# A first stage ordered by a list scheduler, with five more chunks of q in it, and an output projection by input quarters

## The chip, the cores and the metric

The kernel runs on one core of a Trainium2 chip. A core has TensorE (PE, matmuls; its weight loads are listed as PEld), VectorE (DVE), ScalarE (ACT), GpSimd (POOL) and SyncE (SP), each with an instruction stream of its own that it works off strictly in order, and 16 DMA engines fed from queues; here SP's queue carries the weights, POOL's some small transfers. The metric is the device time of one execution in microseconds, the median of several runs. Matmuls accumulate into PSUM, of which the kernel uses eight banks of 128 partitions x 512 float32.

## The reference

One encoder layer over 256 tokens of width 2048, all in float32. Only the attention mixer is used (the depth is 1).

```python
mod = silu(c) @ mod_w + mod_b                          # 2048 x 12288, one row c
sh_m, sc_m, g_m, sh_f, sc_f, g_f = split(mod, 6)
h = x * (1 + sc_m) + sh_m
q, k, v = split(h @ w_qkv + b_qkv)                      # 2048 x 3072: 32 q heads, 8 k and 8 v heads of 64
q, k = rope(q), rope(k)
s = where(|qpos - kpos| <= 128, q @ k.T / 8, -inf)      # four q heads share one k and v head
m = max(s.max(), sink); p = exp(s - m)
o = (p / (p.sum() + exp(sink - m))) @ v
x = layer_norm(alpha * x + (1 + g_m) * (o @ w_o + b_o)) # w_o: 2048 x 2048
h = x * (1 + sc_f) + sh_f
y = square(relu(h @ w1 + b1)) @ w2 + b2                 # 2048 -> 8192 -> 2048
out = layer_norm(alpha * x + (1 + g_f) * y)
```

## The kernel before

**Numbers and chunks.** Every large product is made of three matmuls in a reduced float32 format (`mm3`, L556): the high half of the activation by the high half of the weight (L557), high by low (L558), low by high (L559). Weights come in chunks of 128 x 2048 float32 (1 MB). A chunk of weights is split in two pieces of 1024 columns: ScalarE rounds a piece to the tile `wh` (L291), VectorE takes the difference to the raw chunk, `wl` (L262). The activations hold their halves in `g` tiles (`held`, pairs `hh, hl`).

**Stream.** `Stream` (L218) holds one list of chunks in the order in which they are loaded, all from SP's queue. There are eight raw buffers (`raws`, five, and three early ones, `raws2`, given up later), five `wh` and five `wl` tiles. `loads` asks for the next chunks while buffers are free; `pump` rounds and subtracts ahead as far as the tiles allow; `main` gives the next chunk's halves; `done` marks a half as used. A raw buffer comes free when its second low half is made or, for a chunk of modulation weights, when its product is.

**Modulation.** The 2048 x 12288 product with one row has 96 chunks. A row product puts the chunk through PE (`quad`, L346, PSUM tile `pm`), after which ScalarE copies the row out (`mrow`, L375) and PE turns it (`pt`, L426; for the gate L460 and L462). A column product is one VectorE instruction over the whole chunk (L386; `cb` holds the spread c). `MIXP` says which of the 16 groups of 128 inputs have their scale and shift by rows (ten groups, two chunks each), the rest by columns; `FFP` says it for the feed-forward's four groups. `columns` adds the bias, and `modulated` (L578) makes h of 128 inputs: one ScalarE instruction and two of VectorE.

**First stage.** q, k and v are six columns of 512 outputs (`CORD`): k, q0, v, q1, q2, q3. The first three, `p` = 0 to 2, are 12 chunks, each of four units (`UNITS`: 128 inputs of one column), accumulated in six PSUM banks (`sums`, two token tiles of three columns). Between them stand the 32 chunks of modulation for x. The order is written out by hand as letters: u a unit, g a modulation product, m a `modulated`, p a pump. With `S.pin` set the instructions keep this order on their engines. Each column gets its bias through a matmul (`bq`, L207) and is copied out (`evict`). PE has some instructions without use at the start (`idle`).

**Slots.** The other 12 q chunks (`LATE`, columns q1, q2, q3, four input groups each) run over two banks for a column. Three (`PRE`) come before the first scores, between them the rotation and the transposes of k and q0. Then come 25 slots: 0 to 8 have a q chunk each, 9 to 24 a chunk of the output projection. Slots 0 to 15 also hold one step of attention each, with four heads and one token tile: `scores` (L744), which VectorE masks and reduces (L751) and ScalarE puts through the exponential (L761); `normalise` (L776); `probs_T`, the transposes of the probabilities (L786); and in each second slot `values` (L802, with L806 for the low half). `SLOT_FILL` says how many chunks of modulation (gate rows, then the feed-forward's groups) are placed at each slot.

**Output projection.** `project(js, c)` (L844) makes 512 outputs from two input quarters (`oT[j]`: eight heads), so from two chunks in two slots. The eviction adds the bias (L888) for the first half of the inputs, and for the second adds to the first (L890), multiplies with the gate and adds x (L892 to L895). The last, `c` = 3, runs token tile by token tile, with the statistics and the normalisation behind each (`add_gated` L811, `norm_scalars`, `normed` L837, L842). The gate gets to the rows' form by `m_gm.spread` at slot 13: a row (`grow`, L475) goes out to DRAM (L476) and comes back on all partitions (L478), both by POOL's queue. `project_0(3)` at slot 20 applies it to a part that is done by then. After this comes the feed-forward, with W1 and W2 in four blocks.

## Time and profile before

| | us |
|---|---|
| median of 3 runs | 1116.48 (1114.97 to 1117.6) |
| profiled execution | 1114.57 |
| its span | 1112.8 |
| PE busy in the span | 1071.0 (96%) |
| VectorE busy | 761.2 (68%) |
| ScalarE busy | 522.9 (47%) |
| mean granted clock of PE | 0.986 of full |

The trace is of one execution, and its times count from the span's start. The stages in it: the first ends at 134.9, the first scores start at 156.7, the feed-forward begins at about 373. A row such as "L262 DVE wl<-raw,wh" tells line, engine, output tile and input tiles; "pa" are PSUM banks for products, "pt" for transposes, "pm" for modulation rows, "g" the general tiles of 128 x 1024. In a table of stretches, each engine's busy time stands with the number of its instructions, "PEclk" is the granted clock, "DMA share" how busy the 16 DMA engines were. In a list of waits the numbers are total us, count, and the longest one. Where an instruction's row ends in brackets, they hold the idle time ahead of it and what ended it.

### The profile page before, as it was taken

To read this page: it belongs to the slowest core of one execution; us is meant where nothing else is said; L and a number is where in the kernel's file an instruction comes from. 1 tells how busy PE (TensorE), PEld (TensorE's weight loads), DVE (VectorE), ACT (ScalarE), POOL (GpSimd) and SP (SyncE) were. 2 spreads that over 40 slices of the span, in tenths; PEclk is the share of its full clock that TensorE was granted. 3 is DMA by queue.
4 is the path that set the end of the run, shared out by engine and by line. 5 is a ranking of instruction groups with operands and counts; after the bars stand their busy time and mean duration, and the time that the engine had idled before them with its cause. 6 is when DMAs were issued, how large, how long until landed. Compare 5 with 4: busy or idle time off the path is not lost.

```text
span 1112.8 us, 15919 instructions
## 1 busy us (share of the span) xinstructions
PE 1071.0 (96%) x6377; PEld 880.0 (79%) x6377; DVE 761.2 (68%) x1098; ACT 522.9 (47%) x811; POOL 21.4 (2%) x42
## 2 busy tenths in 40 slices
PE   8887999899999998999999999999999999999995
PEld 5655677677678798988888888888888888888884
DVE  2576688888548687765578878766666556665576
ACT  2333447888743446553444443334444344444340
POOL 2000000000000000000000000000000000000001
PEclk9998999999999999999999999999999999999998
DMA  9999989878697698555677777876555555557522
GB/s 377 419 420 420 419 299 343 305 293 302 227 386 258 272 361 312 189 190 189 229 282 284 294 287 246 304 269 224 190 189 189 189 191 189 188 189 265 189 76 76
DMA packets 43835, 292.74 MB, mean 263 GB/s; under 512 B 5060, under 2 KB 5220, under 8 KB 9968
## 3 DMA queue, kind: packets, MB, share of 16 engines
q1 hardware_dynamic: 40400, 281.83, 68.1%
q0 software_dynamic: 2496, 8.43, 2.4%
q10 hardware_dynamic: 864, 1.45, 0.4%
q8 instruction: 50, 0.82, 0.3%
q14 instruction: 25, 0.20, 0.0%
HBM read 289.58 MB, written 2.11 MB: 262 GB/s over the span
## 4 chain that ended last, share of the span: by engine, by line
PE 83%; DVE 8%; ACT 3%; DMA 3%; issue 2%; POOL 0%; SPq 0%; DVEq 0%; ACTq 0%; POOLq 0%
PE pa L1077 16%; PE pa L558 15%; PE pa L559 14%; PE pa L557 14%; PE pa L1078 8%; PE pm L346 3%; PE pa L1053 3%; DVE wl L262 3%; PE pa L1054 3%; PE pa L1055 3%; DVE raw L386 2%; DMA raw<-in_wqkv 1%; ACT wh L291 1%; PE pa L744 1%; PE pa L802 1%
## 5 line engine op out<-in xcount | busy, mean ns | idle before, releaser
L262 DVE TENSOR_TENSOR wl<-raw,wh 128x1024 fp32r<-128x1024 f32 x332 | 402.6, 1222 | 240.1 <-ACT wh L291 239.0
L291 ACT CAST wh<-raw 128x1024 fp32r<-128x1024 f32 x332 | 346.0, 1051 | 390.0 <-PE pa L559 220.1
L558 PE MATMUL pa<-wl,g 128*128 128x512 f32 x816 | 321.9, 395 | 8.8 <-DVE wl L262 8.5
L557 PE MATMUL pa<-wh,g 128*128 128x512 f32 x816 | 319.6, 397 | 7.6 <-ACT wh L291 5.8
L559 PE MATMUL pa<-wh,g 128*128 128x512 f32 x816 | 319.2, 393 | 0.0
L1077 PE MATMUL pa<-g,wh 128*128 128x512 f32 x768 | 271.6, 399 | 0.0
L1078 PE MATMUL pa<-g,wl 128*128 128x256 f32 x768 | 215.7, 281 | 0.0
L557 PEld LDWEIGHTS pa<-wh,g 128*128 128x128 f32 x816 | 152.5, 188 | 47.9 <-ACT wh L291 8.0
L558 PEld LDWEIGHTS pa<-wl,g 128*128 128x128 f32 x816 | 154.7, 190 | 43.9 <-DVE wl L262 12.5
L559 PEld LDWEIGHTS pa<-wh,g 128*128 128x128 f32 x816 | 154.5, 190 | 33.3 <-issue 0.8
L1077 PEld LDWEIGHTS pa<-g,wh 128*128 128x128 f32 x768 | 144.3, 188 | 36.2 <-issue 0.2
L1078 PEld LDWEIGHTS pa<-g,wl 128*128 128x128 f32 x768 | 145.1, 189 | 0.1
L386 DVE CUSTOM_DVE_ANT_0 raw<-raw,cb 128x2048 f32<-128x2048 f32 x52 | 118.2, 2283 | 10.1 <-DMA raw<-in_mod 10.1
L1053 PE MATMUL pa<-g,wh 128*128 128x256 f32 x256 | 73.0, 288 | 4.5 <-ACT wh L291 4.5
L1055 PE MATMUL pa<-g,wl 128*128 128x256 f32 x256 | 72.8, 287 | 0.1
L1054 PE MATMUL pa<-g,wh 128*128 128x256 f32 x256 | 72.3, 285 | 0.0
L1053 PEld LDWEIGHTS pa<-g,wh 128*128 128x128 f32 x256 | 49.4, 194 | 5.4 <-ACT wh L291 5.4
L1054 PEld LDWEIGHTS pa<-g,wh 128*128 128x128 f32 x256 | 49.2, 193 | 0.9 <-DVE b L914 0.7
L1055 PEld LDWEIGHTS pa<-g,wl 128*128 128x128 f32 x256 | 49.4, 193 | 0.4 <-DVE wl L262 0.3
L346 PE MATMUL pm<-raw,cact 128*32 128x128 f32 (+1 forms) x1024 | 47.0, 324 | 0.9 <-DMA raw<-in_mod 0.8
L346 PEld LDWEIGHTS pm<-raw,cact 128*32 128x32 f32 x1024 | 28.0, 112 | 19.4 <-issue 11.7
L761 ACT ACTIVATE g<-g,nm 128x256 f32<-128x256 f32 x64 | 31.8, 499 | 16.8 <-DVE nm L751 16.7
(180 smaller groups left out, 659.5 us busy)
## 6 DMA issues: line engine op xcount, KB each, us to landing
raw<-in_mod SPq DMA_DIRECT2D x96, 1024.0 KB, 7.9
raw<-in_w SPq DMA_DIRECT2D x64, 1024.0 KB, 4.9
raw<-in_w1b SPq DMA_DIRECT2D x48, 1024.0 KB, 4.9
raw<-in_wqkv SPq DMA_DIRECT2D x24, 1024.0 KB, 12.7
raw<-in_wo SPq DMA_DIRECT2D x16, 1024.0 KB, 7.5
raw<-in_w1a SPq DMA_DIRECT2D x16, 1024.0 KB, 7.2
g<-in_x SPq DMA_DIRECT2D x4, 512.0 KB, 8.5
gb<-in_lnrow POOLq DMA_DIRECT2D x8, 256.0 KB, 5.7
```

What stands on the lines that cost most here:

```text
L262: self.pinned(nc.vector.tensor_sub(l, r, f32(self.hs[n])))
L291: self.pinned(nc.scalar.copy(h, s))
L346: i = nc.tensor.matmul(self.ps[32 * j:32 * j + 32, :w], lhsT[j] if type(lhsT) is list else lhsT, rhs[j], start=self.first, stop=stop)
L386: S.pinned(nc.vector.tensor_tensor_reduce(out=raw, in0=raw, in1=cb, scale=1.0, scalar=0.0, op0=OP.mult, op1=OP.add, accum_out=self.dst))
L557: nc.tensor.matmul(ps, xh, wh, start=start, stop=False)
L558: nc.tensor.matmul(ps, xh, wl, start=False, stop=False)
L559: S.prev = nc.tensor.matmul(ps, xl, wh, start=False, stop=stop).ins
L1053: nc.tensor.matmul(o, wh(w, 128), hh, start=new, stop=False)
L1054: nc.tensor.matmul(o, wh(w, 128), hl, start=False, stop=False)
L1055: nc.tensor.matmul(o, wl(w, 128), hh, start=False, stop=end)
L1077: nc.tensor.matmul(ps, wh(k, 128), hb, start=k == 0, stop=False)
L1078: nc.tensor.matmul(ps[:, :256], wl(k, 128), hb[:, :256], start=False, stop=k == NK - 1)
```

## The change

1. *The first stage's order comes from a list scheduler.* `first_order` has a cost in us for each kind of operation, what each must wait for, and the times at which the loads would land by its own model (2.47 us a chunk, eight buffers). It takes again and again the operation that could start first, and by rank among equals. The kernel then emits the operations in that order, all pinned: g a modulation product, r, c and a the row's copy, transpose and bias, H, T and S the three instructions of `modulated` (T now writes a tile of its own, `xm`), h and l a high and a low half, u a unit, e an eviction, sp and cp the spread of c.
2. *Five more chunks run in it.* `SEQ` has the 12 chunks and, as pairs (input group, column), (0,3), (0,4), (1,3), (1,4), (2,3): three quarters of q1 and two of q2. The modulation rows share one bank (`gv`), which frees the eighth bank for these: a quarter and token tile is accumulated, then evicted, by ScalarE as a copy for group 0 and by VectorE as an addition after it (`add_part`). `spread` uses this bank too.
3. *Seven chunks are left behind it* (`LATE`), two of them ahead of the slots, and there are 21 slots instead of 25: q chunks in slots 0 to 4, the projection in 5 to 20. The later parts of q1 and q2 are added to `acc` on VectorE.
4. *The output projection goes by input quarters,* `project(c, j)`, one chunk and one slot each, j outermost. Each is evicted: j = 0 with the bias (L1058), 1 and 2 by addition, 2 with the gate and x behind it (`project_0`, L1069 and L1070), 3 by `add_gated`, which is now the end of all four columns. The last one has 12 matmuls for each token tile, where 24 stood.
5. *What hangs on slot numbers moves.* The gate's spread goes to slot 11 (was 13), the rows of x to 11 (was 15), the first feed-forward columns to 17 (was 19); `SLOT_FILL` is new. `FFP` becomes (2, 2, 4, 0). The rotary tables are made ahead of the stage.

```diff
-PRE = 3
-OUT_AT = 9
-X_AT = 15
+PRE = 2
+OUT_AT = 5
+X_AT = 11
+SLOT_FILL = (1, 1, 1, 1, 1, 1, 1, 2, 2, 2, 2, 2, 2, 2, 2, 2, 2, 2, 2, 2, 1, 0, 0)
...
-FFP = (0, 4, 4, 0)
+FFP = (2, 2, 4, 0)
...
+SEQ = [(0, [1, 2]), (1, [3]), (2, []), ((0, 3), [4]), ((0, 4), [5]), (3, [6]), (4, [7]), (5, []),
+       ((1, 3), [8]), ((1, 4), [9]), (6, [10]), (7, [11]), (8, [12]), ((2, 3), [13]),
+       (9, [14]), (10, [15]), (11, [])]
...
+def first_order():
+    cost = dict(gP=1.1, gD=2.37, r=.27, c=.3, a=.16, H=.55, T=.42, S=.42, h=1.0, l=1.18, u=1.37, e=.6, sp=.85, cp=.6)
...
+        best = None
+        for key, (eng, d, after, rank) in ops.items():
+            t = engine[eng]
...
+                if best is None or (round(t, 2), rank, ranks[key]) < best[0]:
+                    best = (round(t, 2), rank, ranks[key]), key, t
+        _, key, t = best
+        eng, d, _, _ = ops.pop(key)
+        engine[eng] = t + d
+        done[key] = eng, t + d
+        out.append((t, len(out), key))
+        if key in frees:
+            slots.append(t + d)
+    return [key for _, _, key in sorted(out)]
...
-    LATE = [(g, p) for p in (3, 4, 5) for g in range(4)]
+    LATE = [(3, 3), (2, 4), (3, 4)] + [(g, 5) for g in range(4)]
...
-    OUTS = [(c, js, x) for js in ((0, 1), (2, 3)) for c in range(4) for x in range(2)]
+    OUTS = [(c, j) for j in range(4) for c in range(4)]
...
+    gv = bank("gv")
+    for k, m in enumerate(m_mix):
+        if m.m is not None:
+            m.m.at = lambda k=k: gv[:, k // 2 % 2 * 256:k // 2 % 2 * 256 + 256]
...
+    def quarter(wh, wl, g, p, i):
+        hh, hl = held[g]
+        t = i // 2
+        if i % 2 == 0:
+            quarter_of[g, p, t] = bank()
+        for k in (i % 2 * 2, i % 2 * 2 + 1):
+            s = slice(k * 256 + t * 128, k * 256 + t * 128 + 128)
+            mm3(quarter_of[g, p, t], hh[:, s], hl[:, s], wh(k), wl(k), k == 0, k == 3)
...
+    def add_part(ps, t, c, new):
+        d = acc[c][:, t * 512:t * 512 + 512]
+        if new:
+            S.pinned(nc.scalar.copy(d, ps))
+        else:
+            S.pinned(nc.vector.tensor_add(d, d, ps))
...
-    for n in range(12):
-        u, ms = units(n), list(AHEAD[n])
...
-            steps = ["uuuu", "ugugpumu", "ugugumgugp"][len(ms)]
...
+    for op, *v in first_order():
+        if op == "g":
...
+        S.loads()
...
-    def project(js, c):
+    def project(c, j):
...
+            if j == 0:
                 nc.vector.tensor_add(y, ps, bo(c))
...
+            elif j < 3:
+                nc.vector.tensor_add(y, y, ps)
+            else:
+                add_gated(ps, t, c, g1, st)
+        if j == 2:
+            project_0(c)
...
-    run(qkv(*LATE[2]), [lambda: qT.__setitem__(0, heads_T(qA[0]))])
+    qT[0] = heads_T(qA[0])
...
-        if n == 13:
+        if n == 11:
             g1 = m_gm.spread([g4(), g4()])
```

How it moves instructions is shown at four places; a name with a number is one buffer of a tile, and the line numbers of the rows after the change are those of the changed kernel.

In the first stage PE's stream before, in the second half of the stage, goes from one chunk of units to the next: `wh_778` and `wl_789` are one half of a chunk, `pa_119` to `pa_124` the six banks of `sums`.

```order
L557 MATMUL pa_121<-wh_817,g4_724 128x512
L557 MATMUL pa_122<-wh_817,g4_724 128x512
L558 MATMUL pa_123<-wl_789,g4_724 128x512
L559 MATMUL pa_123<-wh_778,g4_725 128x512
L558 MATMUL pa_124<-wl_789,g4_724 128x512
L559 MATMUL pa_124<-wh_778,g4_725 128x512
L558 MATMUL pa_119<-wl_789,g4_724 128x512
L559 MATMUL pa_119<-wh_778,g4_725 128x512
L558 MATMUL pa_120<-wl_789,g4_724 128x512
L559 MATMUL pa_120<-wh_778,g4_725 128x512
L558 MATMUL pa_121<-wl_821,g4_724 128x512
L559 MATMUL pa_121<-wh_817,g4_725 128x512
```

After the change the same stretch has a quarter (bank `pa_664`, group 0's activations `g4_257` and `g4_258`) between the units of two chunks:

```order
L679 MATMUL pa_664<-wh_541,g4_257 128x512
L680 MATMUL pa_664<-wl_571,g4_257 128x512
L681 MATMUL pa_664<-wh_541,g4_258 128x512
L679 MATMUL pa_664<-wh_541,g4_257 128x512
L680 MATMUL pa_664<-wl_571,g4_257 128x512
L681 MATMUL pa_664<-wh_541,g4_258 128x512
L679 MATMUL pa_121<-wh_618,g4_614 128x512
L680 MATMUL pa_121<-wl_625,g4_614 128x512
L681 MATMUL pa_121<-wh_618,g4_615 128x512
L679 MATMUL pa_122<-wh_618,g4_614 128x512
L680 MATMUL pa_122<-wl_625,g4_614 128x512
L681 MATMUL pa_122<-wh_618,g4_615 128x512
```

PE has matmuls of a q quarter, whose activations were made long before, ahead of units that need the newest group.

VectorE in the same stage before: the two column products of a group (L386), its bias, the two instructions of `modulated` (L586, L587), three of the rotary tables, and only then the low halves of the next chunk.

```order
L386 ISA raw_640,modm_113<-raw_640,cb_111 128x2048
L386 ISA modm_113 128x1
L386 ISA raw_666,modm_113<-raw_666,cb_111 128x2048
L386 ISA modm_113 128x1
L420 TENSOR_TENSOR modm_113<-modm_113,pack_83 128x2
L586 TENSOR_SCALAR g4_553<-g4_553,modm_113 128x256
L587 TENSOR_TENSOR g4_725<-g4_553,g4_724 128x256
L162 TENSOR_SCALAR g4_782<-pack_83,posf_783 128x32 x2
L167 TENSOR_SCALAR g4_782<-g4_782 128x64
L168 TENSOR_SCALAR g4_782<-g4_782 128x64
L262 TENSOR_TENSOR wl_789<-raw_615,wh_778 128x1024
L262 TENSOR_TENSOR wl_821<-raw_697,wh_817 128x1024
```

After, with the changed kernel's lines (L352 the low half, L496 the column product, L710 and L712 `modulated`, L779 the addition of a quarter):

```order
L352 TENSOR_TENSOR wl_787<-raw_601,wh_763 128x1024
L352 TENSOR_TENSOR wl_795<-raw_601,wh_785 128x1024
L496 ISA raw_641,modm_113<-raw_641,cb_112 128x2048
L496 ISA modm_113 128x1
L496 ISA raw_657,modm_113<-raw_657,cb_112 128x2048
L496 ISA modm_113 128x1
L561 TENSOR_TENSOR modm_113<-modm_113,pack_83 128x2
L710 TENSOR_SCALAR xm_839<-g4_639,modm_113 128x256
L352 TENSOR_TENSOR wl_850<-raw_662,wh_837 128x1024
L712 TENSOR_TENSOR g4_842<-xm_839,g4_841 128x256
L352 TENSOR_TENSOR wl_873<-raw_662,wh_852 128x1024
L779 TENSOR_TENSOR g4_569<-g4_569,pa_829 128x512
```

Low halves stand on both sides of the column products, the tables are gone from here, and an addition of 512 columns has come in.

Ahead of the first scores (L744) PE has before, behind q0's transposes (L729), the end of a q chunk and a row product:

```order
L729 MATMUL pt_1366<-ident_85,g4_1170 128x128 x4
L729 MATMUL pt_1372<-ident_85,g4_1170 128x128 x4
L557 MATMUL pa_1221<-wh_1248,g4_724 128x512
L558 MATMUL pa_1221<-wl_1269,g4_724 128x512
L559 MATMUL pa_1221<-wh_1248,g4_725 128x512
L557 MATMUL pa_1221<-wh_1248,g4_724 128x512
L558 MATMUL pa_1221<-wl_1269,g4_724 128x512
L346 MATMUL pm_1194<-raw_1203,cact_106 32x256 x8
L559 MATMUL pa_1221<-wh_1248,g4_725 128x512
L744 MATMUL pa_1396<-g4_1308,g4_1365 128x256
L744 MATMUL pa_1397<-g4_1308,g4_1365 128x256
L744 MATMUL pa_1396<-g4_1308,g4_1365 128x256
```

After (L902 the transposes, L917 the scores) the chunk and the row product stand ahead of the transposes:

```order
L679 MATMUL pa_1471<-wh_1438,g4_1116 128x512
L680 MATMUL pa_1471<-wl_1457,g4_1116 128x512
L681 MATMUL pa_1471<-wh_1438,g4_1117 128x512
L679 MATMUL pa_1471<-wh_1438,g4_1116 128x512
L456 MATMUL pm_1380<-raw_1389,cact_106 32x256 x8
L902 MATMUL pt_1529<-ident_85,g4_1356 128x128 x4
L902 MATMUL pt_1535<-ident_85,g4_1356 128x128 x4
L680 MATMUL pa_1471<-wl_1457,g4_1116 128x512
L917 MATMUL pa_1541<-g4_1499,g4_1528 128x256
L917 MATMUL pa_1542<-g4_1499,g4_1528 128x256
L917 MATMUL pa_1541<-g4_1499,g4_1528 128x256
L917 MATMUL pa_1542<-g4_1499,g4_1528 128x256
```

Between the transposes and the scores one matmul is left of the five and the row product.

In a slot of the projection VectorE has before, at the first half of the inputs, two additions with the bias (L888) in two slots, here with a column product between and the reductions of the scores (L751) behind:

```order
L888 TENSOR_TENSOR g4b_2401<-pa_2252,g4b_2248 128x512
L386 ISA raw_2348,modf_114<-raw_2348,cb_111 128x2048
L386 ISA modf_114 128x1
L888 TENSOR_TENSOR g4b_2401<-pa_2253,g4b_2248 128x512
L262 TENSOR_TENSOR wl_2453<-raw_2210,wh_2387 128x1024
L751 ISA g4_2422,nm_2423<-pa_2416,msk_141,nsnk_104 128x256
L751 ISA nm_2423 128x1
L751 ISA g4_2422,nm_2423<-pa_2417,msk_141,nsnk_104 128x256
```

After, in a slot with j = 2, two additions (L1058) and the gate's four instructions (L1069, L1070), with the reductions (now L924) in the midst:

```order
L352 TENSOR_TENSOR wl_3011<-raw_2738,wh_2950 128x1024
L942 TENSOR_TENSOR rs_2990<-sm_2929,es_2927 128x4
L530 TENSOR_TENSOR modf_114<-modf_114,pack_83 128x2x2
L946 RECIPROCAL rs_2990<-rs_2990 128x4
L1058 TENSOR_TENSOR g4b_2107<-g4b_2107,pa_2936 128x512
L1069 TENSOR_TENSOR g4b_2107<-g4b_2107,g4_2794 128x512
L1058 TENSOR_TENSOR g4b_2107<-g4b_2107,pa_2937 128x512
L1070 SCALAR_TENSOR_TENSOR g4_2286<-g4_2286,g4b_2107 128x512
L1069 TENSOR_TENSOR g4b_2107<-g4b_2107,g4_2794 128x512
L924 ISA g4_3027,nm_3028<-pa_3021,msk_142,nsnk_104 128x256
L924 ISA nm_3028 128x1
L1070 SCALAR_TENSOR_TENSOR g4_2286<-g4_2286,g4b_2107 128x512
```

VectorE has six instructions of 512 columns for the eviction of one chunk here.

More of the change, by code (lines that the diff above doesn't have):

```diff
@@ L369, in step @@
                               last and k == kc - 1)
[L370 to L371 removed]
+            if last and not self.at:
                 self.out()
         def out(self):
[L375 removed]
+            self.r = sml.tile([128, 256], F32, name="mrow", bufs=1)
+            S.pinned(nc.scalar.copy(self.r[:, :self.w], self.ps[:, :self.w]))
     class Col:
```

343 lines of the change are left out of this document (217 added, 126 removed).

## The prediction

> **What bounds the kernel now.** I read the page first, then the busy time of each engine by stretch, then the waits and the rows around the places that change.
>
> ```profile
> span 1112.8 us, 15919 instructions
> PE 1071.0 (96%) x6377; PEld 880.0 (79%) x6377; DVE 761.2 (68%) x1098; ACT 522.9 (47%) x811; POOL 21.4 (2%) x42
> ```
>
> PE stands busy for 96% of the span; the changed stages must be looked at one by one, since 41.8 us of idle time lie somewhere.
>
> ```profile
> core 0: us, PE busy (x) PEld busy (x) DVE busy (x) ACT busy (x) POOL busy (x), PEclk, DMA share, GB/s
> 10.00:134.00 124.00, 105.14 (x957) 78.31 (x958) 73.92 (x112) 41.25 (x63) 0.00 (x0) 0.94 1.01 420
> 134.00:157.00 23.00, 23.00 (x145) 17.07 (x145) 19.96 (x22) 11.27 (x15) 1.14 (x2) 1.00 0.86 326
> 157.00:310.00 153.00, 149.46 (x924) 109.87 (x921) 122.29 (x272) 120.08 (x296) 2.10 (x4) 1.00 0.80 298
> 310.00:373.00 63.00, 62.88 (x419) 47.26 (x418) 42.73 (x65) 17.84 (x21) 0.53 (x1) 1.00 0.72 273
> 373.00:1112.00 739.00, 722.63 (x3893) 621.98 (x3892) 501.20 (x620) 330.97 (x417) 11.48 (x17) 0.99 0.64 227
> ```
>
> The first row is the first stage: the DMA engines are full (share 1.01, 420 GB/s) and PE is not. In the three rows behind it, q, k and v's rest, attention and output projection up to 373 us, PE is full to 3.7 us of 239 and the DMA is not. The waits say the same; first those of PE in 0 to 134 us, then the longest of 134 to 380 us.
>
> ```profile
> PE pa L558 <- DVE wl L262: 8.5, 5, 3.5
> PE pa L557 <- ACT wh L291: 5.8, 6, 1.9
> PE pt L426 <- ACT mrow L375: 2.2, 5, 0.4
> ```
> ```profile
> PE pt L462 <- ACT mrow L460: 2.9, 1, 2.9
> ```
>
> A matmul's duration (0.39 us) overlaps the next one's, so what a chunk costs PE is read from starts: 24 matmuls lie between these two.
>
> ```profile
> 356.25 0.39 PE L557 MATMUL pa<-wh,g 128*128 128x512 f32 x1
> 361.69 0.39 PE L557 MATMUL pa<-wh,g 128*128 128x512 f32 x1
> ```
>
> So a chunk is 5.44 us of PE, 0.227 us a matmul, while its load is 1.0486 MB at 420 GB/s, 2.50 us. Where the load sets the pace a chunk costs 2.50 us; where PE does, 5.44 us. That is what the change plays on.
>
> **The change, part by part.** *(1) Five q chunks leave the stretch that PE fills:* 5 x 5.44 = 27.2 us saved there. Their bias rows and evictions stay.
>
> *(2) The first stage grows.* It ends at the last bias pair, and its first product starts at 7.17:
>
> ```profile
> 7.17 1.08 PE L346 MATMUL pm<-raw,cact 128*32 128x128 f32 x32
> 134.34 0.61 PE L207 MATMUL pa<-g,g 128*128 128x512 f32 x2
> 134.88 1.07 PE L346 MATMUL pm<-raw,cact 128*32 128x256 f32 x16
> ```
>
> It ends at 134.9. Behind the load used at 7.2 come 43 loads of 1.0486 MB and 1.84 MB of x: 46.9 MB at 420 GB/s, 111.7 us, so its last chunk lands at 118.9, and PE is 16.0 us later. After, 48 loads and the same x: 52.2 MB, 124.2 us, landing at 131.4. From below, the last chunk must still be rounded (1.05, L291's mean), subtracted (1.22, L262's) and multiplied (5.44, and 6 bias pairs of 0.45 = 2.7): 10.4 us, an end at 141.8. From the other side, the old lag of 16.0 gives 147.4. PE's own work there is 17 x 5.44 + 20 row products of 1.0 + 2.7 + 16 of broadcast and warm-up, about 131 us from 7.2: an end at 138, so PE could follow but with little to spare. I take the middle, 144.6: +9.7 us. The low halves now stand ahead of the 2.2 us column products, and the rotary tables are out of the way, which speaks against the old lag; the fullness of PE speaks against the lower end. This hides the five chunks under loads: were that cover gone (PE waiting as it did), they would cost their 5.44 again.
>
> The sources of durations in the rest, VectorE and the chain, are these (starts again give what one costs in a row):
>
> ```profile
> 260.33 2.28 DVE L386 CUSTOM_DVE_ANT_0 raw<-raw,cb 128x2048 f32<-128x2048 f32 x1
> 262.53 0.68 DVE L888 TENSOR_TENSOR g4b<-pa,g4b 128x512 f32<-128x512 f32 x1
> 263.13 1.21 DVE L262 TENSOR_TENSOR wl<-raw,wh 128x1024 fp32r<-128x1024 f32 x1
> 264.27 0.48 DVE L751 CUSTOM_DVE_ANT_0 g<-pa,msk,nsnk 128x256 f32<-128x256 f32 x1
> ...
> 265.88 0.68 DVE L806 TENSOR_TENSOR g<-pa,g 128x512 fp32r<-128x512 f32 x1
> ```
> ```profile
> 156.71 1.11 PE pa L744 x8
> 165.49 1.71 ACT g L776 x4
> 196.55 1.00 PE pm L346 x16
> 207.72 1.88 PE pa L802 x16
> 213.62 0.87 PE pt L786 x8
> ```
>
> A column product takes 2.20 us of VectorE, a 512-wide addition 0.60, a low half 1.14, four score reductions 1.61. A row product takes PE 1.00, scores 1.11, the transposes 0.87, values 1.88 for two slots.
>
> *(3) Before the first scores* two chunks stand where three stood, and the second q transpose has no chunk's first half around it. From the stage's end VectorE has 7 low halves (8.0), 2 column products (4.4), two rotations (4 x 0.60 + 1.14 each, 7.1) and 2 additions (1.2): 20.7 us before q is turned. PE has 64 matmuls (14.5), 3 row products (3.0), bias and one transpose (1.8): 19.3. It waits 1.4, and behind the transposes has one matmul before the scores instead of five and a row product: two copies of ScalarE, of which about 0.6 shows. +2, between 0 and 4.
>
> *(4) In slot 0* the way from the scores' start to the last normalised row is 156.71 to 165.49 + 1.71 = 167.20: 10.5 us. What PE has meanwhile falls to 8.1 (scores 1.11 twice, 22 matmuls 5.0, bias 0.9). +2, between 0 and 2.4. A bubble of more than this would need a VectorE that is late as well.
>
> *(5) Evictions.* By halves there were 42 VectorE instructions of 0.60 in the projection (8, 24, and 10 for the last column); by quarters 64 (8, 8, 8 + 16, 24), and 4 more add q's quarters: 26 x 0.60 = 15.6 us more. The 10 low halves that go to stage one take off 11.4. VectorE is busy 185.0 of 239 us between 134 and 373 now, 189 of some 222 after. A full slot asks of it 2.28 + 2.20 + 1.61 + 1.2 + 0.3 (half of L806) + about 0.9 of rotation and 0.3 of small ones = 8.8, of PE 5.44 + 1.11 + 0.87 + 0.94 + 1.00 = 9.4. So VectorE stays below PE, at 94%, and what waits is the odd reduction behind an addition. +3, between 0 and 15.6; nearer to nothing, since 153 - 122.3 = 30.7 us of VectorE are idle in 157 to 310 alone.
>
> *(6) The gate rows.* They are sent at the end of slot 11 and read by VectorE late in slot 13 (before, from slot 13 to about 18). The way through POOL's queue:
>
> ```profile
> 290.63 0.51 POOL L476 DMA_DIRECT2D rowm<-grow  x1 [145.62 <-ACT grow L475]
> 294.25 1.07 POOL L478 DMA_DIRECT2D g<-rowm  x2 [3.12 <-DMA rowm<-grow]
> ```
> ```profile
> g<-rowm POOLq DMA_DIRECT2D x2, 512.0 KB, 11.7
> g<-in_x SPq DMA_DIRECT2D x4, 512.0 KB, 8.5
> ```
>
> 294.3 + 0.5 + 11.7 - 290.6 = 15.9 us, against some 16.4 (a slot of 9.4 and 7 of the next). If late, everything behind `project_0` on VectorE waits, the next slot's reductions first. +1, between 0 and 4. The rows of x (8.5) are asked for at slot 11 and read in slot 13: hidden. SP issues the same loads, POOL the same transfers.
>
> *(7) The last projection* runs over 12 matmuls a half instead of 24, so the two normalisation chains overlap.
>
> ```profile
> 362.57 0.69 DVE L811 TENSOR_TENSOR tmp<-pa,g 128x512 f32<-128x512 f32 x1 [1.05 <-PE pa L559]
> 366.31 0.55 DVE L842 TENSOR_SCALAR g<-g,mv,r 128x512 f32<-128x512 f32 x1
> 368.01 0.69 DVE L811 TENSOR_TENSOR tmp<-pa,g 128x512 f32<-128x512 f32 x1 [1.15 <-PE pa L559]
> 371.74 0.16 DVE L837 SCALAR_TENSOR_TENSOR nmr<-mv,r 128x1 f32<-128x1 f32 x1
> ```
>
> The first chain (4.3 us) ran under 5.4 us of matmuls, and will have 2.7. Its rest pushes the second: +1, between 0 and 1.6. *(8) The 2.9 us wait for `mrow`* may shrink, since four matmuls now stand between product and transpose (4 x 0.227): -1, between -2.9 and 0.
>
> The feed-forward stages, the other 739 us, do the same work; 4 row and 4 column products merely change places between two groups. The sum: -27.2 + 9.7 + 2 + 2 + 3 + 1 + 1 - 1 = -9.5 us. The profiled execution took 1114.57 (span 1112.8 and 1.8 around it), 1.9 below the median of 1116.48; so 1105.1 against it, **1107.0** against the median. The ends together are -27.2 + 6.9 - 2.9 = -23.2 and -27.2 + 12.5 + 27.6 = +12.9.
>
> What the clock adds. PE was granted full clock after its longest wait in the later stages (2.9 us; PEclk 1.00 in 157 to 310), but not in the first stage:
>
> ```profile
> 80.00:90.00 10.00, 4.59 (x13) 3.04 (x13) 7.89 (x13) 2.50 (x3) 0.00 (x0) 0.67 1.01 418
> ```
>
> PE was idle for 5.4 of these 10 us, and 0.67 is what two thirds of the stretch at half the clock would give. The Trainium skill ("TensorE: Matmul & The Clock Gate", "What's actually happening") says that a gap of a window of about 3.4 us halves the clock until a busy window has passed. By that rule terms 3 and 4, if they fell into one gap of 4 us, would cost an estimated 1.7 us more, and the sum would be -7.8; by the row of 2.9 us, nothing. The trace agrees with it on both sides.
>
> The Trainium skill ("DMA: Bandwidth & Descriptors", "Specifications") gives about 358 GB/s for a core's share of HBM. By that the 52.2 MB would take an estimated 146 us, the stage would end some 22 us later than in my sum, and the kernel would be slower than now. The trace disagrees: 420 GB/s over 124 us; so it has no chance of its own here.
>
> **The rivals.** *A, the whole gain:* the schedule holds at its lower end and terms 3 to 8 cover each other: -27.2 + 6.9 + 2 = -18.3, **1098**. For it: PE fills the later slots today to 3.7 us. Against: VectorE at 94% of a slot in strict order.
>
> *B, the change doesn't do what it says:* PE's waits in the first stage stay. They are 124 - 105.14 = 18.9 us today; if the longer stage has as many, it ends at 7.2 + 131 + 18.9 = 157, 22 later than now. Of the 27.2 only 5 are left, and terms 3 to 8 ask 8 of them: 1116.5 + 3 = 1119.5; with a few us of waits less, **1117**. For it: one order fixed beforehand for three engines, and eight raw buffers that a late engine holds. Against: the loads, which set the pace, are asked for in the same way.
>
> *C, slower:* VectorE becomes the bound of the slots with a column product and two evictions. It decides when a slot needs more than 9.4 + 9.5/13 = 10.1 us, in the 13 slots of n = 5 to 17, against the 8.8 worked out. If waits in its order (it waits for scores, for ScalarE's halves) bring it to 10.7, 13 x 1.3 = 16.9 take the place of term 5's 3: **1121**. For it: DVE at 122.3 of 153 us already with a slot of 9.5, and durations a seventh above the starts. Against: ten low halves fewer, and the additions need nothing late.
>
> **How the numbers follow.** A measurement of this kernel can tell about 0.2%, 2.2 us. My case, 1101 to 1114, has 0.68; A 0.12; B 0.11; C 0.09. Of B 0.02 lies below the bound of no change, 0.06 inside and 0.03 above it; C lies above. Faster 0.82, same 0.06, slower 0.12. The range reaches from A's value to B's: 1098 to 1117, leaving out about 0.05 below and, with half of B and C, 0.14 above.
>
> **What would show it.** Step 2: the last bias pair of the first stage at 142 to 148 us, DMA at 420 GB/s to some 131 us, and a granted clock near 1.00 there; an end past 152 makes the forecast wrong. Steps 3 and 4: idle PE of 1 to 2 us before the first scores and before the first transposes of probabilities. Step 5: VectorE above 85% between there and the feed-forward stage, with slots of 9.4 to 9.8 us; slots above 10.1 are C. Step 6: a wait of VectorE in slot 13 on the gate's transfer. Steps 1 to 8 together: the first feed-forward matmul 8 to 11 us earlier, and the rest equal. A feed-forward stage that is longer would be none of these.

## The result and the profile after

The changed kernel takes 1100.18 us (1099.03 to 1104.09), the kernel before 1115.97 beside it: a ratio of 0.9863, 95% interval 0.9835 to 0.9891, so 15.3 us less by the ratio, where 9.5 were forecast. The measured time lies in the forecast range (1098 to 1117), a little under the likeliest case's own (1101 to 1114). The profiled execution took 1099.58 us.

The head of the profile after, and its busy times by the stages that the prediction used (first stage, up to the first scores, slots, feed-forward):

```profile
span 1097.8 us, 16222 instructions
PE 1067.2 (97%) x6505; PEld 879.9 (80%) x6505; DVE 780.0 (71%) x1131; ACT 523.0 (48%) x812; POOL 21.5 (2%) x42
```
```profile
10.00:143.70 133.70, 127.53 (x1081) 99.92 (x1081) 86.97 (x116) 53.85 (x75) 0.00 (x0) 0.99 1.01 420
143.70:165.10 21.40, 21.00 (x134) 15.29 (x133) 20.27 (x23) 8.71 (x13) 0.75 (x2) 1.00 0.98 394
165.10:360.50 195.40, 189.77 (x1361) 137.91 (x1361) 166.52 (x356) 129.09 (x308) 3.03 (x6) 1.00 0.81 301
360.50:1097.00 736.50, 721.49 (x3885) 621.47 (x3885) 500.35 (x618) 329.36 (x415) 11.50 (x17) 0.99 0.64 226
```

For the comparison, the kernel before by its own borders:

```profile
10.00:134.90 124.90, 106.04 (x963) 78.77 (x963) 74.82 (x113) 42.15 (x63) 0.00 (x0) 0.95 1.01 420
134.90:156.70 21.80, 21.80 (x139) 16.33 (x138) 19.06 (x21) 10.37 (x14) 1.14 (x2) 1.00 0.85 322
156.70:375.10 218.40, 213.47 (x1348) 158.00 (x1347) 166.06 (x340) 139.63 (x319) 2.63 (x5) 1.00 0.78 292
375.10:1112.00 736.90, 721.80 (x3886) 621.38 (x3886) 500.16 (x618) 329.26 (x415) 11.48 (x17) 0.99 0.64 226
```

The first stage is 8.8 us longer (its end is 143.7, from 134.9), the stretch up to the scores 0.4 shorter, the slots 23.0 shorter (218.4 to 195.4), the feed-forward equal to 0.4. In the first stage PE's idle time fell from 18.9 to 6.2 us (133.70 - 127.53), at the same 420 GB/s. Its busy time rose by 21.5 us only, though 120 matmuls at 0.227 us are 27.2, with the granted clock up from 0.95 to 0.99: with the holes between chunks gone, matmuls that were there before run faster too. The clock alone gives 4.3 of these 5.7 us, an estimate from the two rows: 106.04 x (1 - 0.95/0.99). VectorE has 16 instructions more in the slots and no more time (166.1 and 166.5 us).

The waits of PE after, first in the first stage, then from the first scores to the feed-forward:

```profile
PE gv L456 <- DMA raw<-in_mod: 2.5, 2, 1.9
PE pa L765 <- ACT cb L863: 1.4, 1, 1.4
PE pa L679 <- ACT g L777: 1.4, 1, 1.4
```
```profile
PE pa L917 <- ACT g L903: 2.6, 1, 2.6
PE pa L1217 <- ACT wh L381: 1.2, 1, 1.2
```

The 8.5 us for low halves and 5.8 for high halves of before are gone from the first stage. What is left is the start (a load), the spread of c through one bank (L765) and one copy of a quarter (L777). In the slots the 2.9 us for `mrow` are gone, and 2.6 for a copy of transposed q (L903) ahead of the scores of slot 8 have come. None of PE's waits in the slots, 5.6 us of idle time together, ends at an eviction of the projection.

### The profile page after: what moved, and what is told of

The parts are those of the page before. It is cut to its first block, busy times and chain, and to the rows that moved or that the text cites. A ratio compares the mean times of both kernels' runs of the same rounds, so it can differ in the third digit from the quotient of the medians.

```text
span 1097.8 us, 16222 instructions
## 1 busy us (share of the span) xinstructions
PE 1067.2 (97%) x6505; PEld 879.9 (80%) x6505; DVE 780.0 (71%) x1131; ACT 523.0 (48%) x812; POOL 21.5 (2%) x42
## 4 chain that ended last, share of the span: by engine, by line
PE 84%; DVE 7%; DMA 4%; issue 2%; ACT 2%; SPq 0%; POOL 0%; DVEq 0%; POOLq 0%; ACTq 0%
PE pa L1241 16%; PE pa L679 15%; PE pa L680 15%; PE pa L681 15%; PE pa L1242 8%; DMA raw<-in_mod 3%; PE pa L1217 3%; PE pa L1218 3%; PE pa L1219 3%; DVE raw L496 3%; PE gv L456 2%; DVE wl L352 2%; PE pm L456 1%; DMA gb<-in_lnrow 1%; PE pt L959 1%
## 5 line engine op out<-in xcount | busy, mean ns | idle before, releaser
L352 DVE TENSOR_TENSOR wl<-raw,wh 128x1024 fp32r<-128x1024 f32 x332 | 403.8, 1222 | 232.1 <-ACT wh L381 214.4
L496 DVE CUSTOM_DVE_ANT_0 raw<-raw,cb 128x2048 f32<-128x2048 f32 x52 | 118.4, 2285 | 16.3 <-DMA raw<-in_mod 10.7
L949 ACT ACTIVATE g<-g,rs 128x256 f32<-128x256 f32 x64 | 27.7, 500 | 10.7 <-DVE rs L946 10.5
```

The costliest lines, as they stand in the source:

```text
L352: self.pinned(nc.vector.tensor_sub(l, r, f32(self.hs[n])))
L496: S.pinned(nc.vector.tensor_tensor_reduce(out=raw, in0=raw, in1=cb, scale=1.0, scalar=0.0, op0=OP.mult, op1=OP.add, accum_out=self.dst))
```

## Experiments

All ratios are against the kernel before, run beside each kernel on the same chip; since its median varied from 1113.7 to 1116.0 between these groups of runs, kernels are compared by ratio. 0.1% is 1.1 us. The three times on the right are us of one profiled execution each, so a difference of 1 to 3 us between two of them can be that of two executions (the last section shows one source).

| kernel | ratio | 95% interval | first stage ends | first scores | first feed-forward matmul |
|---|---|---|---|---|---|
| before | 1 | | 134.9 | 156.7 | 375.1 |
| changed | 0.9863 | 0.9835 to 0.9891 | 143.7 | 165.1 | 360.5 |
| quarters_only | 1.0002 | 0.9993 to 1.0011 | 134.9 | 156.6 | 375.0 |
| sched_12 | 0.9945 | 0.9932 to 0.9957 | 130.1 | 153.1 | 369.5 |
| hand_17 | 1.0084 | 1.0069 to 1.0100 | 173.4 | 194.8 | 387.8 |
| halves | 1.0021 | 1.0012 to 1.0030 | 143.2 | 164.6 | 378.2 |
| four | 0.9880 | 0.9864 to 0.9896 | 140.3 | 163.4 | 363.1 |
| six | 0.9916 | 0.9901 to 0.9931 | 153.4 | 164.9 | 365.9 |
| columns_first | 0.9902 | 0.9888 to 0.9915 | 149.9 | 167.5 | 363.5 |
| cost_one | 0.9907 | 0.9894 to 0.9921 | 147.4 | 168.8 | 365.7 |
| evict_2 | 0.9949 | 0.9936 to 0.9963 | 144.2 | 165.6 | 369.4 |
| evict_3 | 1.0058 | 1.0045 to 1.0071 | 143.6 | 165.0 | 380.5 |
| rope_early | 0.9861 | 0.9849 to 0.9874 | 142.9 | 164.6 | 360.9 |
| turn_first | 0.9821 | 0.9807 to 0.9834 | 143.0 | 164.3 | 356.1 |

The theory going in: the gain is five chunks put under loads, and only an order that keeps PE fed can do that; VectorE's further additions lie beside PE's work. The rivals: the order is worth nothing and any placing of the chunks would do; the additions cost what the prediction charged.

**The output projection by quarters alone** (quarters_only): the kernel before, with `project(c, j)`.

```diff
-    OUTS = [(c, js, x) for js in ((0, 1), (2, 3)) for c in range(4) for x in range(2)]
+    OUTS = [(c, j) for j in range(4) for c in range(4)]
-    def project(js, c):
+    def project(c, j):
```

> The first stage and the 12 late chunks as before; only the output projection goes by input quarters, with its 22 more additions on VectorE, in the same 16 slots. Theory 'covered': PE sets the pace of these slots and VectorE's additions lie beside it, so the time is that of before, 1116 us within 1.5. Rival 'priced': they cost what the prediction put on them, +3 for the evictions and +1 for the last normalisation, about 1120. Rival 'VectorE bound': 22 x 0.60 = 13 us, about 1129.

No difference, to 0.1%. Its slots beside those of before (the quarters first):

```profile
156.60:375.00 218.40, 213.39 (x1348) 158.00 (x1347) 178.20 (x362) 139.45 (x319) 2.64 (x5) 1.00 0.79 292
```
```profile
156.60:375.10 218.50, 213.57 (x1348) 158.06 (x1347) 166.06 (x340) 139.63 (x319) 2.63 (x5) 1.00 0.78 292
```

VectorE has 22 instructions and 12.1 us more, the stretch is 0.1 us shorter. In these slots, of which VectorE is now busy for 82%, the evictions and the shorter last projection cost nothing.

**The scheduler alone** (sched_12): the same, with the list scheduler over the old 12 chunks.

```diff
+SEQ = [(0, [1]), (1, [2, 3]), (2, [4, 5]), (3, [6]), (4, [7]), (5, [8, 9]), (6, [10]), (7, [11]),
+       (8, [12, 13]), (9, [14]), (10, [15]), (11, [])]
+    LATE = [(g, p) for p in (3, 4, 5) for g in range(4)]
```

> The list scheduler orders the first stage, but with the old 12 chunks; 12 late chunks in 3 + 25 slots, the projection by quarters as in quarters_only. Theory 'order': the scheduler alone takes PE's waits out; the last chunk lands at about 119, the first stage ends at 129 to 131 instead of 134.9, and the time is 1111 to 1112. Rival 'fill': PE waited because loads gave it too little work, the order is worth nothing, the stage ends at 134 to 135 and the time is that of quarters_only, about 1116.

The scheduler is worth 0.55%, 6.1 us, and the stage ends at 130.1, as 'order' had it; the time is even a little under its 1111 to 1112. Two things came with the order that no run takes apart from it: the rotary tables are made ahead of the stage, and the modulation rows share one bank. The order could hardly give more, since by the prediction's sum the last chunk's load alone puts the end at 129.3.

```profile
10.00:130.10 120.10, 107.59 (x960) 83.46 (x960) 71.80 (x100) 41.90 (x61) 0.00 (x0) 0.90 1.01 419
```

PE is idle for 12.5 us here, and its clock is 0.90, lower than under the hand-written order (0.95). With 12 chunks PE has too little work under 43 loads.

**The five chunks without the scheduler** (hand_17): the changed kernel, with an order in the old manner.

```diff
-    for op, *v in first_order():
+    for op, *v in hand_order():
...
+        for y, x in enumerate(["uuuu", "ugugpumu", "ugugmugugp"][len(ms)]):
```

> The changed kernel with the same 17 chunks and loads, but the first stage's order written in the manner of the old one (letters by chunk, halves pumped ahead as before) in place of the scheduler's. Theory 'order': PE's waits of before stay beside the five chunks, the first stage ends at 150 to 157 and the time is 1107 to 1114. Rival 'fill': any order that has the chunks in it gets the gain, since PE is nearly full: an end at 144 to 146, and 1100 to 1103.

It is slower than before, by 0.84%, and the stage ends at 173.4, beyond what 'order' expected.

```profile
10.00:173.40 163.40, 142.11 (x1090) 106.74 (x1090) 88.69 (x117) 54.08 (x76) 0.00 (x0) 0.92 0.92 363
```
```profile
PE pa L748 <- DVE wl L420: 9.2, 6, 2.2
PE pa L833 <- ACT cb L931: 3.4, 3, 2.0
```

PE is idle for 21.3 us (18.9 in the kernel before), at a clock of 0.92, and now the loads stop as well: 363 GB/s instead of 420. Buffers are given back late: SP's queue waits in this stage for low halves for 69.0 us, in the changed kernel for 27.9. One of these waits in VectorE's stream, where both column products of a group stand ahead of the half for which PE waits until 80.75:

```profile
75.06 2.28 DVE L564 CUSTOM_DVE_ANT_0 raw<-raw,cb 128x2048 f32<-128x2048 f32 x1
...
77.27 2.29 DVE L564 CUSTOM_DVE_ANT_0 raw<-raw,cb 128x2048 f32<-128x2048 f32 x1
...
79.48 1.22 DVE L420 TENSOR_TENSOR wl<-raw,wh 128x1024 fp32r<-128x1024 f32 x1
```
```profile
80.75 0.50 PE L748 MATMUL pa<-wl,g 128*128 128x512 f32 x1 [1.60 <-DVE wl L420]
```

So the parts don't add: the order alone gives -0.55%, the chunks in the old manner of order +0.84%, both -1.37%. The chunks pay only under an order that feeds PE. This is one order written by hand; a better one was not tried.

**One rank of the scheduler** (columns_first) and **all its costs** (cost_one).

```diff
-                op(g, "DVE", [("m", k, i), ("cp", 3)], 2, "gD")
+                op(g, "DVE", [("m", k, i), ("cp", 3)], 0, "gD")
```

> One number of the list scheduler changed: the column products get rank 0 instead of 2, so among operations that could start at the same time VectorE takes a column product ahead of a low half. Theory 'low halves first': each of the 12 products of 2.2 us now stands at times ahead of a half for which PE waits; the stage ends 3 to 10 us later, 1103 to 1110. Rival 'the greedy order decides': rank only breaks ties, the stage ends within 1 us of 143.7, 1100.

The stage ends at 149.9, 6.2 later, of which 3.0 are left at the feed-forward. The first scores (2.4 later) say less, since 51 weight matmuls stand ahead of them instead of 65 and the rest behind; PE's wait for the copy of transposed q shrinks to 1.0 us. The time is up by 0.39%, with intervals that just overlap, so it is the trace that shows the effect. 'Low halves first' holds, at the lower end of its time.

```diff
-    cost = dict(gP=1.1, gD=2.37, r=.27, c=.3, a=.16, H=.55, T=.42, S=.42, h=1.0, l=1.18, u=1.37, e=.6, sp=.85, cp=.6)
+    cost = dict.fromkeys(("gP", "gD", "r", "c", "a", "H", "T", "S", "h", "l", "u", "e", "sp", "cp"), 1.0)
```

> All costs of the list scheduler set to 1.0 us, so that it takes a column product for as short as a bias addition and a unit for shorter than it is; loads, ranks and rules as they are. Theory 'the costs matter': its order fits no engine, PE waits as in the order written by hand, the stage ends past 150, 1106 to 1120. Rival 'any list order will do': ranks and dependences carry it, an end at 143 to 146, 1099 to 1102.

Between the two: the stage ends at 147.4, 3.7 later, and the time is 0.44% up on the changed kernel's. (The feed-forward begins 5.2 later, but 1.5 of that lie in slot 8 with its slower clock, see the last section.) The numbers matter less than I thought; dependences, buffers and ranks carry most of the order.

**The projection by halves behind the new first stage** (halves).

```diff
-OUT_AT = 5
+OUT_AT = 9
-    def project(c, j):
+    def project(js, c):
```

> The changed kernel with its first stage and seven late chunks, but the output projection by input halves as before, which needs two quarters of heads and so starts at slot 9; slots 5 to 8 have no chunk. Theory 'quarters fill the slots': a slot without a chunk has 4 to 5 us of PE work under a chain from scores to normalised rows of 10.5 us that two slots share, so it takes 6 to 7 us; four of them cost 6 to 10 us, about 1108. Rival 'not needed': the work only moves, and the time stays at 1100 to 1101.

All of the gain is lost, twice what I expected: the feed-forward begins at 378.2 instead of 360.5.

```profile
211.00:249.00 38.00, 25.86 (x172) 15.40 (x172) 27.61 (x74) 27.86 (x80) 0.00 (x0) 0.73 0.74 272
```
```profile
216.47 1.98 PE L976 MATMUL pa<-g,g 128*64 128x256 f32 x8 [4.21 <-ACT g L962]
229.54 2.53 PE L960 MATMUL pt<-ident,g 128*128 128x128 f32 x8 [4.37 <-ACT g L950]
242.77 2.08 PE L918 MATMUL pa<-g,g 64*128 64x256 f32 x8 [3.56 <-ACT g L904]
```

In the slots without a chunk PE is busy for 25.9 of 38 us and waits three times for some 4 us on the chain through ScalarE. Waits are only half of the loss: from the first scores to the feed-forward PE is idle for 14.4 us instead of 5.6, and busy for 199.2 instead of 189.8 with the same work, at a clock of 0.95. So the quarters, which alone are worth nothing, are what lets the seven chunks that are left be enough: a quarter of heads is ready at slot 5, two quarters only at slot 9.

**Four chunks, and six.** `LATE` and the fill of the slots follow.

```diff
-       (6, [10]), (7, [11]), (8, [12]), ((2, 3), [13]),
+       (6, [10]), (7, [11]), (8, [12, 13]),
-PRE = 2
+PRE = 3
```

> The changed kernel with four q chunks in the first stage instead of five; the fifth, (2,3), goes back to the chunks ahead of the first scores, with the second q transpose in its middle as before. Theory 'load against matmuls': PE still has idle time in the first stage, so the fifth chunk costs there only its load, 2.5 of 5.44 us; taking it back ends the stage 2.5 to 4 us earlier and adds 5.44 behind it, less 1 to 2 us of waits ahead of the first scores: 1101 to 1103. Rival 'PE is full at five': the stage gets 5.4 shorter, 1099 to 1100.

The stage ends 3.4 earlier and the feed-forward begins 2.6 later. The difference of the ratios to the changed kernel, 0.17%, is within their intervals. The stage's end is on the side of 'load against matmuls': the chunk costs 3.4 there, not 5.44. What the fifth chunk saves in all is not settled: of the 2.6 us 1.5 lie in slot 8, where the clock was lower in this execution (last section), so about 1 is left.

```diff
-       (6, [10]), (7, [11]), (8, [12]), ((2, 3), [13]),
-       (9, [14]), (10, [15]), (11, [])]
+       (6, [10]), (7, [11]), (8, [12]), ((2, 3), [13]),
+       ((2, 4), [14]), (9, []), (10, [15]), (11, [])]
-PRE = 2
+PRE = 1
```

> The changed kernel with a sixth chunk, (2,4), in the first stage, and one chunk ahead of the first scores instead of two. Theory 'load against matmuls up to PE's limit': PE has 6.2 us of idle time left in the stage, so a sixth chunk still saves 1 to 2.9 us there, but VectorE's 20 us of halves, columns and rotations ahead of the scores lose 5.4 us of cover: no gain, 1100 to 1103. Rival 'more of the same': another 2.9 us, 1097.

Both theories missed: 0.53% slower than with five. The stage ends 9.7 later for one chunk of 5.44.

```profile
PE pa L679 <- DVE g L779: 4.1, 3, 2.6
```
```profile
124.21 2.28 DVE L496 CUSTOM_DVE_ANT_0 raw<-raw,cb 128x2048 f32<-128x2048 f32 x1
...
126.42 2.29 DVE L496 CUSTOM_DVE_ANT_0 raw<-raw,cb 128x2048 f32<-128x2048 f32 x1
...
128.75 0.16 DVE L561 TENSOR_TENSOR modm<-modm,pack 128x2 f32<-128x2 f32 x1
128.95 0.41 DVE L710 TENSOR_SCALAR xm<-g,modm 128x256 f32<-128x256 f32 x1
129.28 0.68 DVE L779 TENSOR_TENSOR g<-g,pa 128x512 f32<-128x512 f32 x1
```
```profile
130.01 0.50 PE L679 MATMUL pa<-wh,g 128*128 128x512 f32 x1 [2.56 <-DVE g L779]
```

The sixth chunk comes right behind the fifth and needs the same single bank, so PE waits for the addition that empties it, which stands behind two column products on VectorE (4.1 us in three waits). The rest is PE's own 5.44, which loads no longer hide. What I feared ahead of the scores, VectorE's 20 us without cover, didn't show: that stretch is 11.5 us with 24 weight matmuls, 0.2 of them idle. The feed-forward begins 5.4 later, and not all of that is the chunk's: 3.0 lie in slot 8, again with a lower clock.

**More evictions** (evict_2, evict_3): one and two more instructions for each eviction of the projection that change nothing in it. In the changed kernel the eviction with the bias is L1056, and those by addition are L1058.

```diff
             if j == 0:
                 nc.vector.tensor_add(y, ps, bo(c))
+            v = part(xs, t, c) if j == 3 else y
+            for _ in range(2):
+                nc.vector.scalar_tensor_tensor(v, ps, 0.0, v, op0=OP.mult, op1=OP.add)
```

> The changed kernel with two instructions of VectorE more for each eviction of the projection (they add zero times the bank to what is there), 60 in all, 0.60 us each, 36 us. Theory 'covered': VectorE needs some 7.9 of the 10.4 us of a slot with attention, so 2.4 us more come to about its end: a cost of 2 to 10 us, 1102 to 1110, much less than 36. Rival 'priced' (every addition shows in part, 3 us for 26): about 7 us by that rate, and then also in the first third of them. Rival 'VectorE already bounds these slots': all 36, about 1136.

> One instruction of VectorE more for each eviction of the projection, 30 of 0.60 us, 18 us. With two more of them (36 us) the kernel was about 22 us slower than the changed one; in that trace the slots with attention were 6.4 us longer for 26 us of additions, the last five 13.8 us for 12. Theory 'two limits': slots with attention have some 2 us of VectorE free each and take 13 us for nothing, while the last slots, without attention, are at their limit and show 5 to 7 us: 1104 to 1107. Rival 'priced per addition': half of the 22 us, 1110 to 1112.

In the changed kernel additions do show: 36 us of them cost 1.95% (21.7 us), 18 us cost 0.86% (9.6 us). The 36 lie far over 'covered' and 'priced' and under the full price; the 18 come near to the half that 'priced per addition' gave. The stretches from slot 5 to slot 15, then from there to the feed-forward, in the changed kernel, with one more and with two more:

```profile
209.40:313.80 104.40, 100.83 (x791) 72.95 (x789) 90.74 (x196) 73.13 (x183) 2.64 (x5) 1.00 0.93 349
313.80:360.50 46.70, 44.91 (x292) 34.07 (x290) 39.91 (x80) 18.51 (x36) 0.00 (x0) 1.00 0.49 175
```
```profile
210.00:318.90 108.90, 102.70 (x792) 73.87 (x790) 100.61 (x213) 72.52 (x183) 2.64 (x5) 0.98 0.90 335
318.90:369.40 50.50, 45.21 (x291) 33.91 (x289) 46.25 (x93) 19.67 (x37) 0.00 (x0) 1.00 0.45 167
```
```profile
209.40:320.20 110.80, 104.70 (x790) 75.64 (x788) 107.46 (x224) 71.61 (x179) 2.64 (x5) 0.97 0.87 318
320.20:380.50 60.30, 49.83 (x292) 34.98 (x290) 56.47 (x112) 20.16 (x39) 0.00 (x0) 0.92 0.43 155
```

With one more, 20 additions (12 us) run in the first stretch, which grows by 4.5: PE's waits for two copies of ScalarE, that of transposed q first, are 2.6 us longer, and slot 8 behind the longer of them runs at a lower clock (0.86, with 12.27 us to the next scores instead of 10.73). The second stretch has 10 (6 us) and grows by 3.8, of which 2.8 are one wait of PE for a low half.

```profile
PE pa L917 <- ACT g L903: 4.2, 1, 4.2
PE pa L975 <- ACT g L961: 1.4, 1, 1.4
```

With two more, 36 of the 40 additions that belong to slots 5 to 14 (21.6 us) run in the first stretch, which grows by 6.4 only. But VectorE, busy for 97% of it, is not done with its work: it ran 224 instructions where 196 and 40 were due. The 12 that are late go over into the last slots, which have 20 additions of their own, and there PE pays at one place. Of the 13.6 us by which that stretch grows, 8.4 are its wait for the low half of the projection's last chunk, which stands behind additions and evictions in a VectorE stream without a gap.

```profile
366.70 0.67 DVE L984 TENSOR_TENSOR tmp<-pa,g 128x512 f32<-128x512 f32 x1
367.29 1.21 DVE L352 TENSOR_TENSOR wl<-raw,wh 128x1024 fp32r<-128x1024 f32 x1
```
```profile
368.56 0.79 PE L680 MATMUL pa<-wl,g 128*128 128x512 f32 x1 [8.38 <-DVE wl L352]
```

So the two stretches don't have a limit each, as 'two limits' took it: what the slots with attention seem to swallow is in part only put off.

**The wait that is left in the slots** (rope_early, turn_first). First the rotation of a q column starts one slot earlier; then, besides, its transposes stand at the start of their slot.

```diff
-            if i == 2:
+            if i == 1:
                 turn = rope(j + 1, 1)
...
+        if j < 3 and i == 3:
+            qT[j + 1] = heads_T(qA[j + 1])
         next(w, None)
```

> The changed kernel with the rotation of each q column begun one slot earlier (steps in the second and third slot of four, transposes in the fourth as before). The longest wait of PE left in the slots, 2.6 us for the copy of the transposed q ahead of a slot's scores, is taken to come from transposes that are late behind the rotation. Theory: the wait goes, 1097 to 1099. Rival 'ScalarE's order': the copy is late because ScalarE has a 1 us high half and two copies of probabilities ahead of it; nothing changes, 1100.

> The rotation one slot earlier, as in rope_early, and the transposes of q at the start of their slot, ahead of its chunk instead of in its middle. Theory: the 2.6 us wait ahead of the scores was for ScalarE's copy standing behind a high half and two copies; with half a chunk and more between, the wait goes, 1097 to 1098. Rival: PE now waits for the copy of probabilities or for VectorE's rotation in the same place, no change, 1099 to 1100.

The rotation alone changes nothing, so VectorE was not what the transposes waited for; 'ScalarE's order' was right. The stream of ScalarE there, in the changed kernel, and the scores that wait for it:

```profile
239.82 1.04 ACT L381 CAST wh<-raw 128x1024 fp32r<-128x1024 f32 x1 [0.72 <-PE pa L681]
240.77 1.06 ACT L961 COPY g<-pt 128x512 f32<-128x512 f32 x2
241.73 1.08 ACT L903 COPY g<-pt 128x512 f32<-128x512 f32 x2
```
```profile
242.38 1.14 PE L917 MATMUL pa<-g,g 64*128 64x256 f32 x8 [2.59 <-ACT g L903]
```

With the transposes first the wait is gone. Slots 5 to 15, here from 208.6:

```profile
208.60:309.50 100.90, 100.42 (x792) 73.28 (x790) 89.62 (x193) 72.45 (x181) 2.64 (x5) 1.00 0.93 359
```

3.5 us less than 104.40, with 0.5 us of idle PE left of 3.6. The kernel has 1094.94 us and a ratio of 0.9821 (0.9807 to 0.9834), 0.42% under the changed one's, with intervals that just don't meet; it is the fastest here. Against rope_early only the place of the transposes differs.

## Why the prediction was right, and where it was off

Direction, range and mechanism held. By its own steps, in the profiled execution (-15.0 us, forecast -9.5):

- *Steps 1 and 2* are right: -27.2 and +9.7 against +8.8. The end of 143.7 lies in the 142 to 148 that the text gave, with the DMA at 420 GB/s and a clock of 0.99. The row of the loads gave the lower end, and it was right to distrust it: sched_12, with PE far from full, ended at 130.1, 1 us over the bound worked out in the same way (118.9 + 10.4 = 129.3), while the changed kernel, with PE nearly full (127.5 of 133.7 us), ended 1.9 over its bound.
- *Step 3*: +2 against about 1.2: ahead of the scores, what is left besides 0.227 us for each weight matmul went from 5.5 (21.8 - 72 x 0.227) to 6.6 (21.4 - 65 x 0.227). Only 0.4 us of it is idle PE, where the text named 1 to 2 as the sign.
- *Steps 4 to 8* fail as a sum: +6 against +2.6. That is what the slots' -23.0 leave when the 113 matmuls that are gone (600 to 487) count 25.6 us. By terms: the bubble of slot 0 (+2) is a wait of 0.3 us ahead of the first transposes of probabilities; the evictions and the last normalisation (+3 and +1) are nothing in quarters_only, but that they are nothing in the changed kernel is not shown: no wait of PE in its slots ends at one of them, yet VectorE is busier there and evict_2's additions do cost; no addition waited for the gate (+1); and the wait for `mrow` went away whole (2.9 instead of 1). On the other side came the 2.6 us for the copy of q, which the text did not have: it looked for what is late next on VectorE, and it was on ScalarE. The feed-forward gave the last 0.4.
- *The test given for VectorE was wrong.* "Slots above 10.1 us are C": they are 104.4 / 10 = 10.4 us, and C did not happen. The 9.4 us left out PE work, not VectorE's: 12 weight matmuls between two of another kind take 2.94 us from start to start (262.98 to 265.92) and not 12 x 0.227 = 2.72, which is 4.4 us in ten slots; two sets of transposes of q and the gate's transposes are some 2 more, and 3.6 us PE is idle. So PE is busy for 100.8 of 104.4 us. The place at which VectorE bounds is 97%, in evict_3.
- *Rival B* is what the change would have been without its scheduler: hand_17 has 21.3 us of idle PE, near to the 18.9 that B put in. But B's 157 left out that the loads stop too and that the clock falls, and the end is 173.4.
- *Rivals A and C.* The time lies between A (1098) and my case. C's mechanism is real and two additions for each eviction away: evict_3 is slower than before, with VectorE as the bound.
- *The clock.* The text put an estimated 1.7 us on one slow stretch by the rule, and nothing by the row of 2.9 us. Behind the new hole of 2.6 us the profiled execution lost nothing, which is luck: four, cost_one and rope_early lost 1.5 us behind the same hole, and six 3.0.

The error is one-sided: the total came out 5.5 us better than the sum, by 0.9 in step 2, 0.8 in step 3, 3.4 in steps 4 to 8 and 0.4 in the feed-forward, and the first feed-forward matmul 14.6 us earlier where 8 to 11 were named. So the time came out 0.8 us under the likeliest case's lower end, in the part of the range that reaches down to A.

What is shown: the gain needs the order, the chunks and the quarters, since each pair without the third was tried and gives -0.55% (no chunks moved), +0.84% (no scheduler) or +0.21% (no quarters). What stays open: what the quarters' evictions cost in the changed kernel's own slots, how near an order written by hand can come, and what decides whether a hole of 2.6 us slows the clock.

## What to carry to other kernels

Work that is moved under loads is worth its whole price less the loads it brings, but only while the order on every engine keeps the bound engine fed; price the move and the order together, since here the one without the other gave two fifths of the gain, the other without the one a loss. When PE fills a stretch, additions on a second engine are free only while that engine keeps up: 12.1 us were free in quarters_only, 18 us cost 9.6 here. An engine that falls behind can pay for it much later and at one place, as in evict_3, so look at what it has not yet done at the end of a stretch. And follow the longest wait that is left to the engine whose queue it stands in, as with the transposes of q, where 3.5 us came from putting three sets of eight transposes, and the rotations ahead of them, earlier. Add up a slot from starts that include the changes from one kind of matmul to another before a limit for it is named.

## What the hardware showed

A hole in PE's work can cost more than its length, since the granted clock can be lower behind it. After 3.56 us of idle PE in halves the eight score matmuls took 2.08 us, where they take 1.14 elsewhere, and the granted clock over those 38 us was 0.73. A hole of 2.6 us goes either way. It stands ahead of the scores of slot 8 in most kernels here, and from these scores to the next PE has the same 88 instructions (89 in turn_first):

| kernel | idle PE ahead of the scores of slot 8, us | us to the next scores | granted clock there |
|---|---|---|---|
| turn_first | none | 10.7 | 1.00 |
| changed, hand_17 | 2.59 | 10.7 | 1.00 |
| four, cost_one, rope_early | 2.59 to 2.60 | 12.2 to 12.3 | 0.86 |
| six | 2.60 | 13.7 | 0.76 |
| evict_2 | 4.17 | 12.3 | 0.86 |

```profile
244.74 2.08 PE L917 MATMUL pa<-g,g 64*128 64x256 f32 x8 [2.60 <-ACT g L903]
```

The row is of six; that of the changed kernel, with 1.14 us after 2.59, stands with the experiment on the transposes. So the same hole cost nothing beyond its length, or 1.5 us, or 3.0. The Trainium skill ("TensorE: Matmul & The Clock Gate", "What's actually happening") puts the window at about 3.4 us. The holes of 3.56 and 4.17 us agree, since the clock was lower behind them. The 2.60 us of six don't, if the window is taken as the least length of a hole, and no run here shows what decided.

The same shows in the first stage: the changed kernel's, with no hole over 2 us, has 0.99, the scheduled one with too little work 0.90. So giving PE more to do made what it had to do cheaper, by 27.2 - 21.5 = 5.7 us in that count, of which the clock is an estimated 4.3.
